# Two-layer hybrid trunk: DeltaNet's triangular solve on VectorE, taps and gates on ScalarE, mixer outputs token-major

## The chip, the cores and the metric

The kernel runs on one core of a Trainium2 chip. The metric is the device time of one execution in microseconds; the median of the runs counts. Engine names follow the profile: PE is TensorE's matmul (PEld its weight load), DVE VectorE, ACT ScalarE, POOL GpSimd, SP SyncE.

## The reference

Two layers of a trunk run on 384 tokens of width 1024: 128 prompt tokens and 256 latents. Each sub-layer is an RMS norm, a shift and scale from a conditioning vector (adaLN), the sub-layer, and a gated residual. Layer 0 mixes with two groups of heads side by side, HGRN2 and gated DeltaNet, both forward and backward; layer 1 is attention. Both end in an MLP of width 4096. What matters here is layer 0's mixer, cut:

```python
q_a, f_fw, f_bw, i_a, g_a, qkv_b, g_b, ... = split(h @ w_in)
f = lb + (1 - lb) * sigmoid(f_raw)                      # HGRN2 forget gates, per direction
o_a = rmsnorm(oa_f + oa_b, gn_a) * silu(g_a)            # HGRN2 output
qkv = silu(short_conv(qkv_b, conv_w))                   # 5 taps, centred
q_b, k_b = l2norm(q_b) * 128**-0.5, l2norm(k_b)
A = where(strict, (k * beta) @ k.T * L, 0)              # in chunks of 32 tokens
u = triangular_solve(I + A, v * beta); w = triangular_solve(I + A, k * beta * exp(g))
o_b = rmsnorm(ob_f + ob_b, gn_b) * silu(g_b)            # DeltaNet output
out = concat(o_a, o_b) @ w_out
```

## The kernel before, in words

**Precision.** Weights arrive as float32 and are split in a high part (`hi`, by ACT, L211) and a low part (`lo` = weight minus `hi`, L212, by DVE or, for blocks listed in `ON_POOL`, by POOL). Each product is three matmuls per 128 rows: hi by hi, hi by lo, lo by hi (L647 to L649 for blocks laid out feature-major, 128x384; L674 to L676 and L689 to L691 for token-major ones, 512 and 256 columns). A block's weights come in two halves of 512 KB through rings of 3 raw, 4 `whi` and 4 `wlo` tiles, so a split waits until TensorE has done with an earlier half.

**Layer 0.** First comes a preparation: the adaLN vectors, the norm, and `fm_group`, which projects the four heads of DeltaNet's keys and the first two forget gates. Then `gdn_prep` makes the 32x32 matrices, and `gdn_solve` (L1038 to L1073) inverts them: it writes them to DRAM and reads them back so that each of 96 matrices lies on a partition (the DMAs into `s` and `sm`), runs 31 steps of two `tensor_tensor` each (L1062 a product, L1063 a subtraction; sizes w(32-w) for w = 1 to 31), and sends the result back through DRAM (`s<-sm`, `hyB<-s`). `gdn_levels` (from L1096) joins the 32-blocks to 128-blocks on TensorE, `gdn_step` (L1146 to L1177) carries the states over the tiles, and `gdn_out` (L1188, L1191) makes the outputs.

**The order.** Each engine runs its instructions in order. A string, `STEPS`, says in which order the pieces are written: `d` advances DeltaNet's chain by a step, `h` HGRN's, `a` adaLN's for later; `f`, `q`, `c`, `v`, `g` are weight blocks for forget gates, queries, conv inputs, HGRN's values and output gates; `m` is the HGRN half of `mix_out`. A scheduler then sets each engine's order from it; `ORDER` holds some matmuls back behind marked ones (`behind`).

**After a block's matmuls** its `evac` runs. For conv (`evac_conv`): two ACT copies, a first tap on DVE (L940), four multiply-adds on DVE (L942), an ACT sigmoid, two POOL products (L950, L951). For forget gates (`evac_f`): an ACT sigmoid, a DVE multiply-add (L717). HGRN's levels are DVE work (L748 to L785, among them L771 and L782) with small matmuls (L747, L759).

**The tail.** The mixers' outputs lie feature-major, 128 features by 384 tokens for each head. `mix_out` squares them (ACT, L1249), sums over features with matmuls against a column of ones (L1251; for DeltaNet also the squares of q, L1255), takes a square root and a reciprocal (L1258, L1259), spreads the result over 128 partitions by matmul (L1263), multiplies and splits in hi and lo (L1265 to L1267). `proj_residual` multiplies with `w_out` (144 matmuls of 512 columns), adds to x (L1273, L1275), `norm` (L528 to L567, transposes L555) prepares the MLP's input, and `mlp` begins (L1340). Tiles go in the order 0 (prompt), 1, 2; the MLP's first two blocks take tiles 0 and 1 first and tile 2 behind.

Of the kernel before, what the change touches and what calls it, by code (L numbers as in the profile page):

```python
# [56 lines left out]
d f3 f1 f2 d q1 a2 q0 d h a2 h a h c4 h a d h3 d c5 h a2 d h v0 h d h d v1 a d h3  # L57
c0 h3 c1 h5 d2 h d2 h d h5 g0 g1 h d h m g2 g3 a3
# [7 lines left out]
ON_POOL = {1: (0, 1), "c5": (0,), "q0": (0,)}  # L66
# [41 lines left out]
class Trunk:  # L108
# [27 lines left out]
    def load_x(self):  # L136
        nc, i = self.nc, self.i
        nc.sync.dma_start(self.x[:, 0], i["x_prompt"][0])
        for t in range(2):
            nc.sync.dma_start(self.x[:, 1 + t], i["x_sample"][0, t * P:(t + 1) * P])  # L140
# [389 lines left out]
    def norm(self, A, B, tag, ready=None):  # L530
# [4 lines left out]
        for t in range(NT):  # L535
# [15 lines left out]
            for j in range(2):  # L551
                pt = self.ps([P, 4, P], "tmp")
                hf = self.sb([P, 4, P], self.tag_hf)
                for k in range(4):
                    self.mark["T", t, j] = nc.tensor.transpose(pt[:, k], xh[j][:, k * P:(k + 1) * P], self.c["ident"])  # L555
# [7 lines left out]
                if j:  # L563
                    self.mark["A", t] = nc.scalar.activation(hi.tiles[j][:, :, c], hf, AF.Copy)
                else:
                    nc.vector.tensor_copy(hi.tiles[j][:, :, c], hf)  # L566
                self.mark["D", t] = nc.vector.tensor_sub(lo.tiles[j][:, :, c], hf, hi.tiles[j][:, :, c].bitcast(F32))  # L567
# [143 lines left out]
    def evac_f(self, d, h):  # L711
        nc = self.nc

        def f(pg):
            s = self.cvt([P, NT, P])
            nc.scalar.activation(s, pg.rearrange("p (t c) -> p t c", t=NT), AF.Sigmoid)
# [124 lines left out]
    def hgrn_out(self, t, r, Sf, Sb):  # L841
# [17 lines left out]
    def mixer_tiles(self):  # L859
# [69 lines left out]
    def evac_conv(self, n):  # L929
# [4 lines left out]
        def f(pg):  # L934
# [5 lines left out]
            nc.vector.tensor_scalar(acc, raw[:, 0:386], w(0), None, op0=ALU.mult)  # L940
# [77 lines left out]

    def gdn_qg(self, t, d):
# [14 lines left out]
    def gdn_solve(self):  # L1034
# [23 lines left out]
        e = nc.gpsimd  # L1058
# [16 lines left out]
    def gdn_levels(self, d):  # L1075
# [65 lines left out]
    def gdn_step(self, t, d, S, want):  # L1141
# [28 lines left out]
        for h in range(4):  # L1170
            self.mark["s", t, d] = nc.tensor.matmul(pu[:, h], kt[:, h], ws[:, h], start=True, stop=True)
# [9 lines left out]
    def gdn_out(self, t, w, S):  # L1181
# [3 lines left out]
        for h in range(4):  # L1185
            for d in range(2):
                last = d == 1 and S is None
                self.mark["out", t] = nc.tensor.matmul(po[:, h], w[d][:, h], self.AT_[:, t, d, h], start=(d == 0), stop=last)  # L1188
            if S is not None:
                for d in range(2):  # L1190
                    nc.tensor.matmul(po[:, h], S[d][:, h], qg[d][:, h], start=False, stop=(d == 1))  # L1191
        nc.scalar.activation(self.vt[:, t], po, AF.Copy)

    def gdn_steps(self):
# [15 lines left out]
        self.gdn_attn()  # L1210
        yield
# [12 lines left out]
    def evac_gate(self, n):  # L1224
# [3 lines left out]
        def f(pg):  # L1228
            s = self.cvt([P, T])
            nc.scalar.activation(s, pg, AF.Sigmoid)  # L1230
            nc.vector.scalar_tensor_tensor(self.sg[:, n], pg, self.prm[:, 12 + n // 4:13 + n // 4], s, op0=ALU.mult, op1=ALU.mult)
        return f

    def mix_out(self, kind, y, tag):
# [570 lines left out]
```

## Time and profile before

| | us |
|---|---|
| median of 3 runs (lowest, highest) | 1165.47 (1164.83, 1169.36) |
| profiled execution | 1165.99 |
| its span | 1164.2 |
| PE busy, share of span | 1102.8 (95%) |
| PEld busy | 940.6 (81%) |
| DVE busy | 766.5 (66%) |
| ACT busy | 493.6 (42%) |
| POOL busy | 286.7 (25%) |

The profile is of one execution with 17957 instructions; the mean granted TensorE clock was 0.978 of full speed. Busy shares are averages over stages of different kinds: the MLP and attention after layer 0's mixer take the larger part of the span, and their share covers what happens in the mixer. The chain of waits and the busy times by stage tell them apart.

### The profile page before, as it was taken

Reading aid. Unit: us, or ns where it says so; the run is one execution under the profiler, and the core shown is the slowest. Engines: PE = TensorE matmul, PEld = TensorE weight load, DVE = VectorE, ACT = ScalarE, POOL = GpSimd, SP = SyncE. Lnnn points to the kernel's source line nnn. Section 1 sums busy time; section 2 is a strip of 40 time slices with the busy share of each in tenths; the row PEclk is TensorE's granted clock in tenths of the full one; section 3 lists DMA queues with packets and bytes.
Section 4 is the critical chain, followed back from the end, with each engine's and each line's share of the span. In section 5 each row is a group of like instructions: output and inputs, shape, how many; then the busy total and the mean of one; then the engine's idle time right before and its main releaser. Section 6 shows DMA issues by size and latency. Waiting matters only on the chain.

```text
span 1164.2 us, 17957 instructions
## 1 busy us (share of the span) xinstructions
PE 1102.8 (95%) x6853; PEld 940.6 (81%) x6853; DVE 766.5 (66%) x1179; ACT 493.6 (42%) x845; POOL 286.7 (25%) x309
## 2 busy tenths in 40 slices
PE   6989978998899799999999999999988999999998
PEld 3868767987866698988988878888767889999987
DVE  4587699895253788885899574877757773333333
ACT  4465323442452564334334353665635543333331
POOL 0054993231210302111112133433003011111102
PEclk9989988998998899999999999999999999999999
DMA  8954625341133287776777317665623964434301
GB/s 292 281 173 110 212 94 160 103 129 35 48 127 115 73 321 246 269 234 202 234 237 222 98 34 196 177 192 143 171 74 97 340 196 139 123 118 127 109 37 55
DMA packets 142090, 184.65 MB, mean 159 GB/s; under 512 B 36803, under 2 KB 113685, under 8 KB 142005
## 3 DMA queue, kind: packets, MB, share of 16 engines
q1 hardware_dynamic: 141685, 183.44, 50.5%
q8 instruction: 54, 0.88, 0.3%
q14 instruction: 31, 0.25, 0.1%
q10 hardware_dynamic: 320, 0.07, 0.0%
HBM read 171.53 MB, written 4.61 MB: 151 GB/s over the span
## 4 chain that ended last, share of the span: by engine, by line
PE 73%; DMA 7%; DVE 7%; POOL 7%; SPq 2%; issue 2%; ACT 1%; DVEq 0%; POOLq 0%; ACTq 0%
PE tmp L1341 7%; PE tmp L1342 7%; PE tmp L1340 7%; PE acc L1326 7%; PE acc L1327 7%; PE acc L1328 7%; POOL sm L1062 2%; POOL sm L1063 2%; DMA ada<-in_ada_w 2%; PE acc L647 2%; PE acc L648 2%; PE acc L649 2%; PE acc L675 2%; PE acc L674 2%; PE po L1715 2%
## 5 line engine op out<-in xcount | busy, mean ns | idle before, releaser
L212 DVE TENSOR_TENSOR wlo<-raw,whi 128x1024 fp32r<-128x1024 f32 x192 | 240.7, 1264 | 167.1 <-ACT whi L211 161.0
L211 ACT ACTIVATE whi<-raw 128x1024 fp32r<-128x1024 f32 x198 | 206.2, 1050 | 334.1 <-PE acc L1328 202.8
L1360 POOL TENSOR_TENSOR h<-h 128x384 f32<-128x384 f32 x56 | 66.9, 1195 | 426.4 <-ACT h L1357 423.7
L1327 PE MATMUL acc<-wlo,h 128*128 128x512 f32 x380 | 148.6, 391 | 0.0
L1326 PE MATMUL acc<-whi,h 128*128 128x512 f32 x380 | 146.1, 393 | 0.0
L349 DVE SCALAR_TENSOR_TENSOR adc<-adr,scz,adc 128x1024 f32<-128x1024 f32 x98 | 126.8, 1323 | 11.7 <-DMA adr<-in_ada_w 11.6
L1328 PE MATMUL acc<-whi,h 128*128 128x512 f32 x380 | 121.2, 391 | 0.0
L1326 PEld LDWEIGHTS acc<-whi,h 128*128 128x128 f32 x380 | 71.2, 188 | 19.7 <-ACT whi L211 5.0
L1340 PE MATMUL tmp<-hyA,whi 128*128 128x384 f32 (+1 forms) x256 | 83.8, 333 | 3.2 <-DVE hyA L566 3.2
L1341 PE MATMUL tmp<-hyA,whi 128*128 128x384 f32 (+1 forms) x256 | 84.8, 332 | 0.4 <-DVE hyA L567 0.4
L1340 PE MATMUL tmp<-hyB,whi 128*128 128x384 f32 (+1 forms) x256 | 83.7, 329 | 1.2 <-DVE hyB L566 1.2
L1341 PE MATMUL tmp<-hyB,whi 128*128 128x384 f32 (+1 forms) x256 | 84.0, 329 | 0.7 <-DVE hyB L567 0.7
L1342 PE MATMUL tmp<-hyA,wlo 128*128 128x384 f32 (+1 forms) x256 | 84.6, 332 | 0.0
L1327 PEld LDWEIGHTS acc<-wlo,h 128*128 128x128 f32 x380 | 71.4, 188 | 14.5 <-DVE wlo L212 0.8
L1342 PE MATMUL tmp<-hyB,wlo 128*128 128x384 f32 (+1 forms) x256 | 82.1, 328 | 0.0
L1328 PEld LDWEIGHTS acc<-whi,h 128*128 128x128 f32 x380 | 71.0, 188 | 13.7
L647 PE MATMUL acc<-hyA,whi 128*128 128x384 f32 x208 | 73.8, 355 | 1.4 <-DVE hyB L708 1.4
L648 PE MATMUL acc<-hyA,whi 128*128 128x384 f32 x208 | 71.9, 345 | 0.0
L649 PE MATMUL acc<-hyA,wlo 128*128 128x384 f32 x208 | 71.3, 344 | 0.0
L1361 DVE TENSOR_TENSOR h<-h,h 128x384 fp32r<-128x384 f32 (+2 forms) x72 | 38.4, 535 | 41.1 <-POOL h L1360 40.4
L1340 PEld LDWEIGHTS tmp<-hyA,whi 128*128 128x128 f32 x256 | 48.4, 191 | 4.5 <-ACT km L562 3.6
L1341 PEld LDWEIGHTS tmp<-hyA,whi 128*128 128x128 f32 x256 | 49.0, 191 | 1.6 <-DVE hyA L567 0.6
(464 smaller groups left out, 2402.5 us busy)
## 6 DMA issues: line engine op xcount, KB each, us to landing
raw<-in_w_mlp SPq DMA_DIRECT2D x128, 512.0 KB, 3.9
adr<-in_ada_w SPq DMA_DIRECT2D x80, 512.0 KB, 4.6
raw<-in_w_in_ab SPq DMA_DIRECT2D x34, 512.0 KB, 5.1
ada<-in_ada_w SPq DMA_DIRECT2D x32, 256.0 KB, 5.3
raw<-in_w_qkv_na SPq DMA_DIRECT2D x32, 256.0 KB, 3.5
raw<-in_w_out_ab SPq DMA_DIRECT2D x8, 512.0 KB, 5.3
m<-gs SPq DMA_DIRECT2D x8, 512.0 KB
raw<-in_w_qkv_na SPq DMA_DIRECT2D x8, 512.0 KB
```

The lines of the kernel that those rows point to most:

```text
L211: self.nc.scalar.activation(hi, x, AF.Copy)
L212: (eng or self.nc.vector).tensor_tensor(lo, x, hi.bitcast(F32), op=ALU.subtract)
L349: nc.vector.scalar_tensor_tensor(acc[v], raw, s[v], acc[v], op0=ALU.mult, op1=ALU.add)
L647: nc.tensor.matmul(pg[n], whi(k)[:, c], hhi[:, k], start=(k == 0), stop=False)
L648: nc.tensor.matmul(pg[n], whi(k)[:, c], hlo[:, k], start=False, stop=False)
L649: nc.tensor.matmul(pg[n], wlo(k)[:, c], hhi[:, k], start=False, stop=(k == KT - 1))
L1326: nc.tensor.matmul(pg, shi, w2hi(n)[:, o], start=start, stop=False)
L1327: nc.tensor.matmul(pg, shi, w2lo(n)[:, o], start=False, stop=False)
L1328: nc.tensor.matmul(pg, slo, w2hi(n)[:, o], start=False, stop=last)
L1340: nc.tensor.matmul(pg[n], w1hi(k)[:, c], hhi[:, k, tc_], start=(k == 0), stop=False)
L1341: nc.tensor.matmul(pg[n], w1hi(k)[:, c], hlo[:, k, tc_], start=False, stop=False)
L1342: nc.tensor.matmul(pg[n], w1lo(k)[:, c], hhi[:, k, tc_], start=False, stop=(k == KT - 1))
```

## The change

It has six parts.

1. In `gdn_solve` the 62 operations go from POOL to DVE (L1062, L1063 before; L1070, L1071 after).
2. First taps (L940 before, L936 after), the forget gates' multiply-add (L717, L716) and the copies into `XT` at the start of `gdn_levels` (L1084, L1092) go from DVE to ACT.
3. POOL makes the lo part of the first halves of f1, f3, f2 and q1 too, besides those of c5, q0 and one MLP block.
4. `STEPS` is written anew: the value conv blocks c4, c5 go first, c0 and c1 later; all four gate blocks stand ahead of `m`.
5. `hgrn_out` and `gdn_out` swap the operands of their matmuls, so that outputs come token-major. A new `out_norm` norms each tile at once (squares summed along the row by ACT, the root on POOL by `pow`, a DVE product). The q part of DeltaNet's norm is made ahead in `gdn_eps`. `mix_out` is called for each tile: four transposes, a DVE product with the gates, ACT hi, DVE lo.
6. The projection, the norm behind it and the first MLP take the tiles in the order 2, 1, 0; DeltaNet's `mix_out` stands between the two halves of the projection's first two tiles (`late`), since `w_out`'s first half multiplies HGRN's outputs alone.

The diff, cut:

```diff
-d f3 f1 f2 d q1 a2 q0 d h a2 h a h c4 h a d h3 d c5 h a2 d h v0 h d h d v1 a d h3
-c0 h3 c1 h5 d2 h d2 h d h5 g0 g1 h d h m g2 g3 a3
+d3 c4 f1 f3 d a2 c5 f2 d a2 q1 q0 d h a h c0 h a h d h3 c1 d h a2 h d v0 h d h d v1 h a d h3
+d h3 d h5 d2 h d2 h d h7 g0 g1 d2 m g2 g3 a3
...
-ON_POOL = {1: (0, 1), "c5": (0,), "q0": (0,)}
+ON_POOL = {1: (0, 1), "f1": (0,), "f3": (0,), "c5": (0,), "f2": (0,), "q1": (0,), "q0": (0,)}
...
-            nc.vector.tensor_scalar(self.G[:, :, d, h], s, self.lb1[:, h:h + 1], self.lb[:, h:h + 1],
-                                    op0=ALU.mult, op1=ALU.add)
+            nc.scalar.activation(self.G[:, :, d, h], s, AF.Identity, scale=self.lb1[:, h:h + 1], bias=self.lb[:, h:h + 1])
...
-            nc.vector.tensor_scalar(acc, raw[:, 0:386], w(0), None, op0=ALU.mult)
+            nc.scalar.activation(acc, raw[:, 0:386], AF.Copy, scale=w(0))
...
-        e = nc.gpsimd
+        e = nc.vector
         for j in range(31):
...
-            nc.vector.tensor_copy(XT[r, :, d, :, r], self.XTc[d][r])
+            nc.scalar.activation(XT[r, :, d, :, r], self.XTc[d][r], AF.Copy)
...
-                self.mark["out", t] = nc.tensor.matmul(po[:, h], w[d][:, h], self.AT_[:, t, d, h], start=(d == 0), stop=last)
+                self.mark["out", t] = nc.tensor.matmul(po[:, h], self.AT_[:, t, d, h], w[d][:, h], start=(d == 0), stop=last)
...
-        nc.scalar.activation(self.vt[:, t], po, AF.Copy)
+        self.out_norm(1, t, po, self.vt[:, t])
...
+    def out_norm(self, kind, t, po, out):
+        nc = self.nc
+        ss, rs = self.sb([P, 4], "ss4"), self.sb([P, 4], "ss4")
         for h in range(4):
+            nc.scalar.activation(out[:, h], po[:, h], AF.Square, scale=P ** -0.5, accum_out=ss[:, h:h + 1])
+        if kind:
+            nc.vector.tensor_add(ss, ss, self.qe[:, t])
+        else:
+            nc.vector.tensor_scalar(ss, ss, EPS * P, None, op0=ALU.add)
+        self.rsqrt(rs, ss)
+        nc.vector.tensor_mul(out, po, rs.unsqueeze(2).broadcast_to([P, 4, P]))
...
+    def mix_out(self, kind, t, y, tag):
...
+            nc.tensor.transpose(pt[:, h], o[:, h], self.c["ident"])
+        v = self.g2([P, 4, P])
+        nc.vector.tensor_mul(v, pt, self.gates_of(kind)[:, :, c])
+        hi, lo = (y[n].tiles[kind][:, :, c] for n in range(2))
+        nc.scalar.activation(hi, v, AF.Copy)
+        nc.vector.tensor_sub(lo, v, hi.bitcast(F32))
...
+        if late:
+            for k in range(2):
+                for t in order[:2]:
+                    for c in range(2):
+                        parts[c](pg[c, t], k, t)
+                if k == 0:
+                    for t in order:
+                        late(t)
```

How it moves instructions is seen at three places. The first is the solve. On POOL, before, with the middle of the solve and the lo half of a weight block among it (`sm4` are the solve's matrices, `wlo` a lo half):

```order
L1063 TENSOR_TENSOR sm4_139_850<-sm4_139_850,sm4_140_851 96x23x9
L1062 TENSOR_TENSOR sm4_140_851<-sm4_138_845,sm4_139_850 96x220
L1063 TENSOR_TENSOR sm4_139_850<-sm4_139_850,sm4_140_851 96x22x10
L1062 TENSOR_TENSOR sm4_140_851<-sm4_138_845,sm4_139_850 96x231
L212 TENSOR_TENSOR wlo_265_1806<-raw_262_1801,whi_264_1805 128x1024
L1063 TENSOR_TENSOR sm4_139_850<-sm4_139_850,sm4_140_851 96x21x11
L1062 TENSOR_TENSOR sm4_140_851<-sm4_138_845,sm4_139_850 96x240
L1063 TENSOR_TENSOR sm4_139_850<-sm4_139_850,sm4_140_851 96x20x12
```

The same part of the solve on DVE, after (`hyB<-cv,acc` is a query block's product with its sigmoid, L707):

```order
L1070 TENSOR_TENSOR sm4_140_851<-sm4_138_845,sm4_139_850 96x256
L210 TENSOR_TENSOR wlo_252_1660<-raw_248_1653,whi_251_1659 128x1024
L1071 TENSOR_TENSOR sm4_139_850<-sm4_139_850,sm4_140_851 96x16x16
L1070 TENSOR_TENSOR sm4_140_851<-sm4_138_845,sm4_139_850 96x255
L1071 TENSOR_TENSOR sm4_139_850<-sm4_139_850,sm4_140_851 96x15x17
L1070 TENSOR_TENSOR sm4_140_851<-sm4_138_845,sm4_139_850 96x252
L1071 TENSOR_TENSOR sm4_139_850<-sm4_139_850,sm4_140_851 96x14x18
L1070 TENSOR_TENSOR sm4_140_851<-sm4_138_845,sm4_139_850 96x247
L1071 TENSOR_TENSOR sm4_139_850<-sm4_139_850,sm4_140_851 96x13x19
L1070 TENSOR_TENSOR sm4_140_851<-sm4_138_845,sm4_139_850 96x240
L707 TENSOR_TENSOR hyB_100_651<-cv_245_1645,acc_243_1595 128x3x128
L1071 TENSOR_TENSOR sm4_139_850<-sm4_139_850,sm4_140_851 96x12x20
```

The solve's operations have left POOL's queue and stand in DVE's, with lo halves and products of the weight blocks between them; L707's product, which was DVE's before too, now stands behind half of the solve.

The second place is what TensorE has in hand just before the solve's result is used (L1096 before, L1104 after, matmuls of 32x32). Before, HGRN's values (256 columns) were the last thing ahead of it:

```order
L690 MATMUL acc_329_2209<-whi_325_2201,hyA_14_129 128x256
L691 MATMUL acc_329_2209<-wlo_326_2202,hyA_13_128 128x256
L689 MATMUL acc_329_2209<-whi_325_2201,hyA_13_128 128x256
L690 MATMUL acc_329_2209<-whi_325_2201,hyA_14_129 128x256
L691 MATMUL acc_329_2209<-wlo_326_2202,hyA_13_128 128x256
L1096 MATMUL gd_142_927<-hyB_98_649,m12_120_753 32x32 x12
L1096 MATMUL gd_143_940<-hyB_98_649,m12_120_753 32x32 x12
L956 MATMUL tmp_273_1876<-ident_73,cv_272_1873 128x128 x3
```

After, it is the conv blocks c0 and c1 (384 columns, into `acc_283` and `acc_315`), with HGRN's first small matmuls (L745) about it:

```order
L647 MATMUL acc_283_1826<-hyA_16_131,whi_280_1821 128x384
L648 MATMUL acc_283_1826<-hyA_15_130,wlo_281_1822 128x384
L646 MATMUL acc_315_2069<-hyA_13_128,whi_311_2061 128x384
L647 MATMUL acc_315_2069<-hyA_14_129,whi_311_2061 128x384
L745 MATMUL hg_289_1902<-hyB_100_651,km_288_1900 32x32 x9
L1104 MATMUL gd_142_927<-hyB_98_649,m12_120_753 32x32 x12
L1104 MATMUL gd_143_940<-hyB_98_649,m12_120_753 32x32 x12
L745 MATMUL hg_289_1902<-hyB_100_651,km_288_1900 32x32 x7
```

All of the values' matmuls and nearly all of HGRN's levels now stand behind the first use of the solve. From the end of `gdn_prep` to there TensorE now has 290 matmuls of 384 columns and 18 of the adaLN's; behind it, up to the last output, 238 of 384 columns (192 before), 144 of 256 (36 before), 240 instructions of the small L757 (L759 before).

The third place is the end of the mixers on TensorE. Before, the last state update (L1171) is followed by a sum of squares (L1251) and by a gate block:

```order
L1188 MATMUL gd_462_3087<-m12_121_754,sm4_420_2849 128x128
L1171 MATMUL gd_424_2860<-g2_423_2858,g2_422_2856 128x128 x4
L1251 MATMUL hg_468_3120<-g2_469_3121,one0_3115 32x384
L647 MATMUL acc_488_3176<-hyA_13_128,whi_484_3168 128x384
L648 MATMUL acc_488_3176<-hyA_14_129,whi_484_3168 128x384
L649 MATMUL acc_488_3176<-hyA_13_128,wlo_485_3169 128x384
```

After, HGRN's last output (L845 to L848) is followed by the transposes of HGRN's normed outputs (L1265, from `hyB_100`) and at once by the projection (L673 to L675, 128x512):

```order
L845 MATMUL hg_458_3024<-hyB_99_650,hyB_100_651 128x128
L847 MATMUL hg_458_3024<-m12_102_653,hq_269_1758 128x128
L848 MATMUL hg_458_3024<-hq_437_2924,hq_269_1758 128x128
L1265 MATMUL hg_485_3186<-ident_73,hyB_100_651 128x128 x4
L673 MATMUL acc_573_3648<-whi_521_3392,hyB_481_3182 128x512
L1265 MATMUL hg_487_3195<-ident_73,hyB_100_651 128x128 x4
L1265 MATMUL hg_489_3204<-ident_73,hyB_100_651 128x128 x4
L674 MATMUL acc_573_3648<-whi_521_3392,hyB_482_3183 128x512
L675 MATMUL acc_573_3648<-wlo_522_3393,hyB_481_3182 128x512
```

The gate blocks have moved ahead of the outputs, and the matmuls of the norms' sums are gone.

More of the change, by code (lines that the diff above doesn't have):

```diff
@@ L134, in banks, with load_x @@
         self.bank = {tag: list(b) for tag, b in tags.items()}
[L136 to L140, printed above, removed]
+    def load_x(self, order=(0, 1, 2)):
+        i = self.i
+        for t in order:
+            self.nc.sync.dma_start(self.x[:, t], i["x_sample"][0, (t - 1) * P:t * P] if t else i["x_prompt"][0])
     @contextmanager
@@ L528, in rsqrt, with norm @@
         self.nc.gpsimd.tensor_tensor(out, x, self.eps[:, 4:5].broadcast_to(list(out.shape)), op=ALU.pow)
-    def norm(self, A, B, tag, ready=None):
+    def norm(self, A, B, tag, ready=None, order=(0, 1, 2)):
         nc = self.nc
@@ L534, in norm @@
         hi, lo = self.split_tiles(tag)
-        for t in range(NT):
+        for n, t in enumerate(order):
             if ready:
@@ L1017, in gdn_attn, with gdn_eps @@
                 nc.vector.tensor_mul(self.AT_[:, t, d], pk, self.AT_[:, t, d])
+    def gdn_eps(self):
+        nc = self.nc
+        pq = self.ps([P, NT, 4], "gd")
+        for h in range(4):
+            q2 = self.g2([P, NT, P])
+            nc.scalar.activation(q2, self.kq[:, :, h, 1], AF.Square, scale=(EPS * P) ** 0.5)
+            for t in range(NT):
+                nc.tensor.matmul(pq[:, t, h:h + 1], q2[:, t], self.c["ones"][:, 0:1], start=True, stop=True)
+        self.qe = self.mixc([P, NT, 4], "qe")
+        nc.vector.tensor_scalar(self.qe, pq, EPS * EPS * P, None, op0=ALU.add)
     def gdn_qg(self, t, d):
@@ L1170, in gdn_step @@
         for h in range(4):
-            self.mark["s", t, d] = nc.tensor.matmul(pu[:, h], kt[:, h], ws[:, h], start=True, stop=True)
+            nc.tensor.matmul(pu[:, h], kt[:, h], ws[:, h], start=True, stop=True)
         S2 = W[:, 1]
@@ L1297, in proj_residual, with mlp @@
         return step
-    def mlp(self, l, hh, fine=()):
+    def mlp(self, l, hh, fine=(), order=(0, 1, 2)):
         nc, i = self.nc, self.i
         hhi, hlo = hh
-        acc = [[self.ps([P, 512], "acc") for _ in range(2)] for _ in range(NT)]
+        acc = {t: [self.ps([P, 512], "acc") for _ in range(2)] for t in order}
         NB = DFF // 256
@@ L1370, in mlp @@
             if b < BEHIND:
-                first((0, 1))
+                first(tuple(sorted(order[:2])))
                 behind.append(first)
@@ L1374, in mlp @@
                     for f in behind:
-                        f((2,))
+                        f(order[2:])
             else:
@@ L1477, in layer0 @@
                 yy = Halves(y[0::2]), Halves(y[1::2])
-                self.mix_out(0, yy, "hg")
+                for t in range(NT):
+                    self.mix_out(0, t, yy, "hg")
         self.pump(100)
@@ L1482, in layer0 @@
         self.open("spo", wo=3, xh=4)
-        self.banks(acc=(2, 3, 4, 5, 0), tmp=(6, 1), mix=(7, 6))
-        self.mix_out(1, yy, "mix")
-        self.load_x()
-        step = self.proj_residual(i["w_out_ab"][0], yy, scr, (("wo", "wo"), ("wo", "m12")))
-        hh = self.norm(*m2, "hyA", step)
+        self.banks(acc=(2, 3, 4, 5, 0, 7), tmp=(6, 1))
+        order = 2, 1, 0
+        step = self.proj_residual(i["w_out_ab"][0], yy, scr, (("wo", "wo"), ("wo", "m12")), order,
+                                  lambda t: self.mix_out(1, t, yy, "tmp"))
+        self.load_x(order)
+        hh = self.norm(*m2, "hyA", step, order)
         self.dump("x0", self.x)
```

77 lines of the change are left out of this document (28 added, 49 removed), and 9 rows, old and new, of the table ORDER.

## Prediction

> **What bounds the kernel now.** I read the profile page first. Its chain that ended last, shared out by engine and then by line, looks like a kernel bound by TensorE:
>
> ```profile
> PE 73%; DMA 7%; DVE 7%; POOL 7%; SPq 2%; issue 2%; ACT 1%; DVEq 0%; POOLq 0%; ACTq 0%
> PE tmp L1341 7%; PE tmp L1342 7%; PE tmp L1340 7%; PE acc L1326 7%; PE acc L1327 7%; PE acc L1328 7%; POOL sm L1062 2%; POOL sm L1063 2%; DMA ada<-in_ada_w 2%; PE acc L647 2%; PE acc L648 2%; PE acc L649 2%; PE acc L675 2%; PE acc L674 2%; PE po L1715 2%
> ```
>
> The MLP lines (L1326 to L1342) make up most of it, and the change hardly touches them. What stands out is GpSimd (POOL), 7% in a kernel of matmuls, on L1062 and L1063: the triangular solve. So I took the chain of waits in order of time, to find where the solve begins and ends (columns: start, length, what):
>
> ```profile
> 106.78 4.57 DMA s<-g
> ...
> 116.78 1.11 POOL sm L1062
> ...
> 177.25 0.68 POOL sm L1063
> ...
> 185.72 5.32 DMA hyB<-s
> 191.09 1.60 PE gd L1096 x48
> ...
> 316.55 0.89 PE gd L1171 x8
> ```
>
> These rows cut layer 0 into stages: preparation until 106.8, a DMA round trip that lays the matrices out for the solve, the solve from 116.8 to 181, a round trip back, the DeltaNet chain from 191.1 to 316.4, and a tail until the MLP begins at 397.9. Busy time by stage:
>
> ```profile
> core 0: us, PE busy (x) PEld busy (x) DVE busy (x) ACT busy (x) POOL busy (x), PEclk, DMA share, GB/s
> 60.00:106.80 46.80, 42.63 (x220) 32.94 (x219) 41.17 (x69) 26.13 (x57) 23.50 (x21) 0.93 0.42 132
> 106.80:116.80 10.00, 10.00 (x61) 8.91 (x60) 2.73 (x4) 6.54 (x9) 3.45 (x4) 1.00 0.69 160
> 116.80:181.00 64.20, 51.13 (x532) 41.15 (x531) 54.32 (x60) 19.27 (x33) 59.84 (x72) 0.90 0.46 152
> 181.00:191.10 10.10, 9.46 (x121) 9.08 (x120) 8.00 (x14) 4.14 (x7) 1.64 (x3) 0.82 0.73 177
> 191.10:316.40 125.30, 116.86 (x1227) 104.66 (x1228) 85.39 (x156) 43.73 (x73) 32.70 (x37) 0.96 0.28 84
> 316.40:397.90 81.50, 74.90 (x306) 51.80 (x305) 43.51 (x62) 36.01 (x61) 15.75 (x13) 0.94 0.31 100
> 397.90:1164.20 766.30, 747.69 (x4060) 655.78 (x4060) 501.26 (x732) 330.58 (x558) 143.26 (x139) 1.00 0.54 169
> ```
>
> In the solve's stage POOL is busy 59.84 of 64.2 us and TensorE 51.13 at a clock of 0.90: TensorE is being given filler. The profiled execution took 1165.99 us, 1.8 more than its 1164.2 span and 0.5 above the runs' median of 1165.47; I sum against 1165.99. About 6 us (0.5%) is what a measurement can tell from no change.
>
> **The solve on VectorE.** The rows that price it, first POOL's, then DVE's in the solve's stage, in the chain's stage, and two sizes from both:
>
> ```profile
> L1062 POOL TENSOR_TENSOR sm<-sm,sm 96x31 f32<-96x31 f32 (+15 forms) x31 | 25.9, 836 | 8.4 <-DMA sm<-s 6.3
> L1063 POOL TENSOR_TENSOR sm<-sm,sm 96x31 f32<-96x31 f32 (+15 forms) x31 | 24.8, 800 | 2.2
> L212 POOL TENSOR_TENSOR wlo<-raw,whi 128x1024 fp32r<-128x1024 f32 x4 | 9.6, 2390 | 17.6 <-ACT whi L211 17.6
> ```
>
> ```profile
> L212 DVE TENSOR_TENSOR wlo<-raw,whi 128x1024 fp32r<-128x1024 f32 x7 | 11.8, 1682 | 15.0 <-ACT whi L211 15.0
> L771 DVE TENSOR_TENSOR x<-x,m 128x512 f32<-128x512 f32 x9 | 11.3, 1272 | 0.0
> ```
>
> ```profile
> L942 DVE SCALAR_TENSOR_TENSOR cv<-cr,prm,cv 128x386 f32<-128x386 f32 x20 | 13.0, 652 | 0.1
> L212 DVE TENSOR_TENSOR wlo<-raw,whi 128x1024 fp32r<-128x1024 f32 x10 | 12.1, 1218 | 6.7 <-ACT whi L211 6.5
> L771 DVE TENSOR_TENSOR x<-x,m 128x512 f32<-128x512 f32 x12 | 8.2, 689 | 0.1
> ```
>
> ```profile
> L785 DVE TENSOR_TENSOR m<-m 128x8 f32<-128x8 f32 x3 | 0.5, 153 | 0.0
> L1273 DVE TENSOR_TENSOR g<-acc,m 128x512 f32<-128x512 f32 x6 | 4.1, 688 | 8.0 <-PE acc L676 8.0
> ```
>
> On POOL the 62 operations take 50.7 us, and strangers queued among them the rest of 64.2. On DVE an operation costs 0.145 us and 1.06 ns per element (from 153 ns at 8 and 688 at 512 elements). The solve's sizes w(32-w), twice for w from 1 to 31, add up to 10,912 elements: 62 x 0.145 + 11.6 = 20.6 us, and I add 3 for handing over between dependent operations. DVE runs in order, and the order puts among them eight conv multiply-adds (8 x 0.652 = 5.2), five lo halves (5 x 1.218 = 6.1) and three products of q (1.6 by the 512-element row): 12.9. Sum 36.5; with some waiting of the lo halves for ACT I take 40. Bounds are 35 and 55, the upper one if every DVE operation is stretched as L771 is from 689 to 1272 ns.
>
> L771 is a hint of that stretch: in the solve's stage, beside a busy POOL, it took 1.85 times as long. The Trainium skill ("SBUF — State Buffer", section "Who interferes with whom") says that a DVE instruction with two SBUF inputs contends with a GpSimd instruction that reads SBUF, and that one fully blocks the other. By that rule the solve gains twice, since what stretched DVE was the solve itself, but pays again wherever POOL's remaining lo halves fall into it; the 689 against 1272 ns agree.
>
> The round trips of 10.0 and 10.1 us stay. The result's DMAs sit on SP's queue behind weight loads, and now wait there for DVE instead of POOL; the loads ahead need slots that the same lo halves free, so I see no new wait of over 2 us.
>
> **TensorE under the solve.** TensorE runs in order, so what stands ahead of the first level (L1096, now L1104) must be done too. Its prices are spacings of starts (columns: start, length):
>
> ```profile
> 328.10 0.33 PE L648 MATMUL acc<-hyA,whi 128*128 128x384 f32 x1
> 328.27 0.33 PE L649 MATMUL acc<-hyA,wlo 128*128 128x384 f32 x1
> 328.45 0.33 PE L647 MATMUL acc<-hyA,whi 128*128 128x384 f32 x1
> ```
>
> ```profile
> 193.36 0.28 PE L689 MATMUL acc<-whi,hyA 128*128 128x256 f32 x1
> 193.48 0.28 PE L690 MATMUL acc<-whi,hyA 128*128 128x256 f32 x1
> ```
>
> ```profile
> 377.21 0.39 PE L676 MATMUL acc<-m,hyB 128*128 128x512 f32 x1
> 377.44 0.40 PE L674 MATMUL acc<-whi,hyB 128*128 128x512 f32 x1
> ```
>
> ```profile
> 311.36 1.05 PE L1156 MATMUL gd<-g,m 128*128 128x128 f32 x8
> ```
>
> ```profile
> L759 PE MATMUL hg<-hq,km 128*32 128x32 f32 x256 | 4.3, 214 | 4.0 <-DVE hyB L750 2.9 <-DVE hyB L773 1.1
> ```
>
> That is 0.175 us for 384 columns, 0.12 for 256, 0.23 for 512, 0.11 for a 128-column record (1.05 less 0.16 of pipeline end, over 8; an instruction leaves two) and 0.017 for one of 32. From the end of preparation to L1104 the new order has 290 of 384 columns (50.8), 18 of the adaLN's 512 (4.1), 9 transposes (2.0) and 41 small ones (1.4): 58.3 us, at a clock of 0.95 about 62. The chain beside it is 10.0 + 40 + 10.1 = 60. I take 62 where 84.3 was.
>
> On that clock: the rows show 0.90 and 0.82 while TensorE was fed thinly, 0.96 and 1.00 when full. The Trainium skill ("TensorE: Matmul & The Clock Gate", Part 1) says that a busy array gets the full clock back within some 3.4 us and an idle one half of it. By that rule the denser stage runs near 1.00, and 58 us would replace the 62.
>
> **Preparation.** First taps and forget gates go to ACT, and two more lo halves to POOL. The rows:
>
> ```profile
> L944 ACT ACTIVATE cv<-cv 128x386 f32<-128x386 f32 x12 | 6.3, 522 | 18.2 <-DVE cv L942 18.1
> L716 ACT ACT_TABLE_LOAD x2 | 2.6, 1283 | 0.0
> L211 ACT ACTIVATE whi<-raw 128x1024 fp32r<-128x1024 f32 x34 | 35.9, 1058 | 43.4 <-PE acc L648 31.4 <-DMA raw<-in_w_in_ab 6.6 <-PE acc L690 3.9
> ```
>
> A tap costs about 0.52 on ACT, busy only 26.13 of 46.8 us there. Two table loads and a POOL half of 2.39 instead of 1.22 on DVE may fall on the path: between 0 and +5, I take +2 (108.8).
>
> **The chain's stage.** Work that lay under the solve has to go here: by the order 46 more of 384 columns (8.1), 108 more of the values' 256 (13.0), 256 more small records of the HGRN levels (4.4), 12 transposes of outputs (2.6) and the few of the q norms: 29 us. If all of it adds, 125.3 + 29 = 154. Dense, the stage holds 238 x 0.175 + 144 x 0.12 + 220 x 0.22 + 734 x 0.017 + some 12 for the rest = 132 us. TensorE was idle 8.4 of 125.3 by its busy time; I let half of that be filled: 150. DVE's share stays under it: 85.4, some 21 moved here without stretch, 8 added by norms and gates, 6 gone to ACT, in all 108.
>
> **The tail.** The 96 gate matmuls (16.8) are gone from it, and so are the sums, broadcasts and square roots of the mixers' norms. What stays: 144 matmuls of 512 columns (33.1), 12 and 16 transposes (6.2), and the norm's two waits, which no edit removes:
>
> ```profile
> 383.07 1.30 PE L555 MATMUL tmp<-ident,xh 128*128 128x128 f32 x5 [2.68 <-DVE ss L546]
> 397.93 0.48 PE L1340 MATMUL tmp<-hyA,whi 128*128 128x256 f32 x2 [3.18 <-DVE hyA L566]
> ```
>
> Sum 45.2. DeltaNet's norm and gate are covered by the first half of the projection, which needs only HGRN's outputs (72 x 0.23 = 16.6 us); without that cover they cost about 5. Bounds 42 and 50; I take 45. Tiles 2, 1, 0 instead of 0, 1, 2 I cost at nothing, since the MLP's first two blocks again run two tiles ahead of the third.
>
> **The sum.** 108.8 + 62 + 150 + 45 = 365.8 against 397.9: 32 us less, 1165.99 - 32.1 = 1134.
>
> **The rivals.** *The solve is stretched by contention.* POOL's halves of f2, q1 and q0 (2.39 each), conv products and hi splits that come late make 55 us of it: 75 instead of 62 in that stage, so 1147. For it: L771's row, and the lo halves' 15.0 us of waiting for ACT. Against: with the solve gone POOL has little to read. The rule of the Trainium skill's "SBUF — State Buffer", "Who interferes with whom", is this rival's mechanism. Chance 0.17. *TensorE fills all gaps.* The chain's stage is near its dense content, 133 instead of 150: 1117. For it: much of what moves here is filler that waits for nothing. Against: DeltaNet's chain was no shorter before. Chance 0.13. *Slower: solve and weights go in lockstep.* The DVE queue holds lo halves between the solve's operations; each waits for ACT's hi, whose slot TensorE frees, which waits for lo halves. If that is serial, a block takes 1.06 + 2.39 + 1.68 + 24 x 0.175 + 3.1 (four taps and a sigmoid) = 12.4 us, and six blocks 75: the stage takes 95, not 62, the chain's stage its full 154, preparation 3 more: 1134 + 33 + 4 + 3 = 1174. It decides once the solve takes about 74 us. For it: DVE has no slack to reorder, and HGRN's levels, which ran beside the solve (the nine L771 above), now stand behind it. Against: four slots let two blocks be split ahead. Chance 0.12.
>
> **How the numbers follow.** The forecast has the remaining 0.58. The range goes from the second rival and a faster tail, 1112, to the first with the upper bounds of preparation, tail and chain, 1162; it leaves out the lockstep. Faster by over 0.5%: 0.58 + 0.17 + 0.13, less 0.07 for upper ends that come within 0.5%: 0.81; same 0.07; slower 0.12.
>
> **What would show it.** In the new profile L1070 and L1071 stand on DVE with means near 0.3 us, and from the first to the last some 40; the first L1104 comes about 62 us after preparation's end, and the MLP's first matmul near 366. Wrong would be: DVE waiting for hi halves among L1070 (lockstep), L1070 means above 0.5 (contention), or an MLP start after 390.

## The result and the profile after

The changed kernel takes 1153.98 us (median of 6 runs, 1149.13 to 1158.77) where the kernel before took 1166.03 (6 runs): a ratio of 0.9891, 95% interval 0.9863 to 0.9919. It is faster by about 12 us, where 32 were forecast. All ratios below are to the kernel before, run in the same group on the same chip, with disturbed runs left out.

Differences to the changed kernel are less certain than the intervals say. The kernel before took 1166 us in the group of the changed kernel's runs and 1170 to 1171 (medians) in the later groups, in which the changed kernel was not run again, so a difference taken from two ratios can be off by some 4 us. A profile shows one execution: the stage behind the MLP's start, the same code in all, varied from 766.3 to 775.0 us between profiles.

The profiled execution took 1153.83 us, 1.8 more than its span. Its busy times by stage, cut at the same events as before (result of preparation sent to DRAM, solve begun, solve ended, first level, last DeltaNet output, MLP under way):

```profile
core 0: us, PE busy (x) PEld busy (x) DVE busy (x) ACT busy (x) POOL busy (x), PEclk, DMA share, GB/s
60.00:116.20 56.20, 42.02 (x203) 32.42 (x202) 47.23 (x65) 33.85 (x73) 32.11 (x29) 0.85 0.36 120
116.20:124.20 8.00, 8.00 (x49) 7.93 (x48) 1.37 (x2) 4.91 (x7) 3.22 (x4) 1.00 0.45 93
124.20:165.60 41.40, 40.69 (x237) 33.60 (x236) 39.52 (x80) 19.21 (x29) 12.55 (x9) 1.00 0.59 191
165.60:177.30 11.70, 9.49 (x119) 8.23 (x118) 9.94 (x17) 3.96 (x7) 0.02 (x1) 1.00 0.84 240
177.30:325.20 147.90, 142.69 (x1654) 130.45 (x1655) 103.50 (x186) 63.61 (x115) 34.84 (x36) 0.97 0.31 96
325.20:383.00 57.80, 46.66 (x217) 38.52 (x215) 32.53 (x56) 24.65 (x68) 17.13 (x11) 0.90 0.36 116
383.00:1152.00 769.00, 748.99 (x4056) 658.23 (x4056) 498.59 (x730) 329.48 (x556) 143.48 (x138) 0.99 0.53 167
```

Beside the forecast's terms, in us:

| stage | before | forecast | after |
|---|---|---|---|
| until preparation's end | 106.8 | 108.8 | 116.2 |
| round trip, solve, round trip | 84.3 | 62 | 61.1 |
| DeltaNet's chain | 125.3 | 150 | 147.9 |
| tail | 81.5 | 45 | 57.8 |
| rest | 766.3 | 766.3 | 769.0 |

Two terms carry the miss: preparation, 7.4 us over the forecast, and the tail, 12.8 over. The two terms in between came out within 2.1 us. The first matmul of the first level shows what ended the second term (start, length, what, idle time before it and its cause):

```profile
177.27 2.52 PE L1104 MATMUL gd<-hyB,m 32*32 32x32 f32 x48 [2.21 <-DMA hyB<-s]
```

TensorE had done what stands ahead of it and waited 2.21 us for the solve's result. It was busy 58.2 of the 61.1 us, at a clock of 1.00: the chain through the solve set the stage, and TensorE's own work was nearly as long.

**The solve.** VectorE's groups in the solve's stage (count, busy us, mean ns, idle time before):

```profile
L1071 DVE TENSOR_TENSOR sm<-sm,sm 96x31 f32<-96x31 f32 (+15 forms) x31 | 15.2, 490 | 0.7
L1070 DVE TENSOR_TENSOR sm<-sm,sm 96x31 f32<-96x31 f32 (+15 forms) x31 | 14.2, 459 | 0.8
```

29.4 us of busy time, where 20.6 had been worked out, with 3 more for handing over. The excess is in a few long operations. One of them, with what POOL did at that moment (start, length, what):

```profile
130.18 0.33 DVE L1071 TENSOR_TENSOR sm<-sm,sm 96x175 f32<-96x175 f32 x1
130.54 2.48 DVE L1070 TENSOR_TENSOR sm<-sm,sm 96x192 f32<-96x192 f32 x1
133.06 0.50 DVE L1071 TENSOR_TENSOR sm<-sm,sm 96x192 f32<-96x192 f32 x1
```

```profile
130.41 2.40 POOL L210 TENSOR_TENSOR wlo<-raw,whi 128x1024 fp32r<-128x1024 f32 x1 [6.32 <-ACT whi L209]
```

An operation of 192 elements, 0.35 us elsewhere, lasts until the lo half that began 0.13 us earlier on POOL is done. It is not slowed by a factor; it stands. That is the rule of the Trainium skill, "SBUF — State Buffer", section "Who interferes with whom", in its strict form, and the 2.48 beside 2.40 us agree with it. Two such stops behind lo halves make about 4.2 of the 8.8 us of excess, and three operations of 1.40 to 1.51 us beside POOL's products L739 about 3.1.

**The preparation.** VectorE's conv multiply-adds in it, before and after:

```profile
L942 DVE SCALAR_TENSOR_TENSOR cv<-cr,prm,cv 128x386 f32<-128x386 f32 x15 | 12.5, 835 | 0.4
```

```profile
L938 DVE SCALAR_TENSOR_TENSOR cv<-cr,prm,cv 128x386 f32<-128x386 f32 x23 | 24.2, 1051 | 3.1 <-ACT cv L936 2.5
```

Eight more, those of c4, and each longer: 11.7 us. (With POOL's old list of lo halves, a run below, the 23 take 18.7 us, so nearly half of the 11.7 goes with the new list.) Moving the first taps away saved VectorE about 0.5 us each. TensorE waits in that stage:

```profile
PE acc L646 <- ACT cv L715: 6.6, 1, 6.6
PE tmp L952 <- POOL cv L946: 4.1, 1, 4.1
```

The first wait is for PSUM. A forget gate's sigmoid has to free it, and in ACT's queue that sigmoid stands behind c4's, which waits 5.4 us for c4's multiply-adds on VectorE and then for a load of ACT's table (1.28 us; eight of them in this stage, six before).

**The tail.** From TensorE's and ACT's timelines around DeltaNet's last output (at the end of a line: idle time before it, and what ended it):

```profile
280.93 1.14 PE L845 MATMUL hg<-hyB,hyB 128*128 128x128 f32 x8
```

```profile
325.24 0.28 ACT L1250 ACTIVATE hyB<-gd 128x128 f32<-128x128 f32 x1 [2.19 <-PE gd L1196]
326.26 0.29 ACT L1250 ACTIVATE hyB<-hg 128x128 f32<-128x128 f32 x1
328.61 1.01 POOL L526 TENSOR_TENSOR ss<-ss,eps 128x4 f32<-128x4 f32 x1 [0.94 <-DVE ss L1254]
330.49 0.46 PE L845 MATMUL hg<-hyB,hyB 128*128 128x128 f32 x2 [4.01 <-DVE ss L1254]
338.73 0.79 PE L673 MATMUL acc<-whi,hyB 128*128 128x512 f32 x1 [3.26 <-ACT hyB L1269]
```

TensorE began HGRN's outputs (L845) at 280.9 and had two of the three tiles done at 291.4. ACT squares the first of them at 326.3, right after DeltaNet's last output, because ACT's queue held HGRN's squares behind DeltaNet's. Until then the two PSUM banks of HGRN stay taken, so the third tile's outputs wait until 330.5, and the projection, which takes that tile first, begins at 338.7, 13.5 us after DeltaNet's last output.

### The profile page after: what moved, and what is told of

Its sections match the earlier page's. It is cut to its first block, busy times and chain, and to the rows that moved or that the text cites. A ratio compares the mean times of both kernels' runs of the same rounds, so it can differ in the third digit from the quotient of the medians.

```text
span 1152.0 us, 18017 instructions
## 1 busy us (share of the span) xinstructions
PE 1088.1 (94%) x6861; PEld 945.6 (82%) x6861; DVE 762.0 (66%) x1216; ACT 507.2 (44%) x904; POOL 249.7 (22%) x243
## 4 chain that ended last, share of the span: by engine, by line
PE 80%; DVE 8%; DMA 5%; ACT 3%; issue 2%; POOL 1%; SPq 1%; DVEq 0%; ACTq 0%; POOLq 0%
PE tmp L1358 8%; PE tmp L1359 8%; PE tmp L1357 7%; PE acc L1343 7%; PE acc L1344 7%; PE acc L1345 7%; DMA ada<-in_ada_w 2%; DVE cv L938 2%; PE acc L1623 2%; PE acc L1624 2%; PE acc L1625 2%; PE acc L648 2%; PE acc L646 2%; PE acc L647 2%; PE acc L673 2%
## 5 line engine op out<-in xcount | busy, mean ns | idle before, releaser
L210 DVE TENSOR_TENSOR wlo<-raw,whi 128x1024 fp32r<-128x1024 f32 (+1 forms) x188 | 229.1, 1228 | 150.9 <-ACT whi L209 142.0
L646 PE MATMUL acc<-hyA,whi 128*128 128x384 f32 x208 | 75.6, 364 | 9.1 <-ACT cv L715 6.6
L647 PE MATMUL acc<-hyA,whi 128*128 128x384 f32 x208 | 72.8, 350 | 0.0
L1378 DVE TENSOR_TENSOR h<-h,h 128x384 fp32r<-128x384 f32 (+2 forms) x72 | 37.8, 526 | 41.4 <-POOL h L1377 40.8
L646 PEld LDWEIGHTS acc<-hyA,whi 128*128 128x128 f32 x208 | 41.1, 198 | 16.8 <-ACT cv L715 7.0
L1358 PEld LDWEIGHTS tmp<-hyA,whi 128*128 128x128 f32 x256 | 49.5, 193 | 3.3 <-DVE hyA L566 2.3
```

Of the source, the lines that this page charges most:

```text
L210: (eng or self.nc.vector).tensor_tensor(lo, x, hi.bitcast(F32), op=ALU.subtract)
L646: nc.tensor.matmul(pg[n], whi(k)[:, c], hhi[:, k], start=(k == 0), stop=False)
L647: nc.tensor.matmul(pg[n], whi(k)[:, c], hlo[:, k], start=False, stop=False)
L1358: nc.tensor.matmul(pg[n], w1hi(k)[:, c], hlo[:, k, tc_], start=False, stop=False)
```

## The experiments

Thirteen kernels. The first two asked what the solve is worth, the next two undid one suspected loss each. The scheduler orders all engines anew for each edit, so two kernels can differ in more than the lines shown.

**The solve back on GpSimd, all else as changed.**

```diff
-        e = nc.vector
+        e = nc.gpsimd
```

> The changed kernel with the solve back on GpSimd, all else as changed. Theory 1 (the solve is worth what its stage shows, and what was lost was lost in the preparation and in the tail): the stage from its first to its last operation goes from 41.4 back to some 60 us, since nothing else on the path covers it: 1170 to 1177 us. Theory 2 (TensorE's moved filler is now the bound under the solve, so that the engine of the solve matters little): under 8 us slower than the changed kernel, at most 1162 us.

Ratio 0.9984 (0.9960 to 1.0008), 0.0093 or 11 us above the changed kernel: between the two theories. Its stages, and its first level:

```profile
116.80:124.30 7.50, 7.50 (x44) 7.42 (x44) 0.60 (x1) 4.42 (x7) 2.49 (x2) 0.98 0.50 96
124.30:190.30 66.00, 60.80 (x529) 51.73 (x528) 45.07 (x49) 30.11 (x48) 61.64 (x74) 1.00 0.51 160
199.20:337.90 138.70, 134.96 (x1482) 121.04 (x1483) 93.09 (x168) 57.24 (x103) 29.66 (x34) 0.94 0.31 93
```

```profile
199.18 1.01 PE L1104 MATMUL gd<-hyB,m 32*32 32x32 f32 x15 [11.03 <-DMA hyB<-s]
```

The solve takes 24.6 us more, as in theory 1, but the chain's stage takes 9.2 less, since HGRN's levels now run beside the solve on a free VectorE (529 matmul records under the solve, not 237). TensorE waits 11.03 us for the solve's result, so TensorE's filler, theory 2's bound, is not the bound here; what halves the gain is that hidden work changes its place.

**The kernel before, with the solve alone on VectorE** (the same line the other way).

> The kernel before with only the solve moved to VectorE. Theory 1: DVE has HGRN's levels beside the solve there, so it gets less than the 23 us of the changed kernel, some 10 to 18: 1148 to 1156 us. Theory 2 (the solve only pays together with the new order of blocks; alone it pushes HGRN's levels back by what it wins): within 6 us of the kernel before, 1160 to 1172 us.

Ratio 1.0021 (0.9998 to 1.0045): theory 2. Its solve and its chain:

```profile
117.50:209.60 92.10, 85.91 (x1045) 72.28 (x1044) 88.07 (x177) 37.28 (x63) 24.68 (x20) 0.98 0.54 171
221.70:316.00 94.30, 77.14 (x767) 71.29 (x767) 51.70 (x95) 26.80 (x43) 16.95 (x17) 0.95 0.12 37
```

On VectorE the solve takes 92.1 us, longer than GpSimd's 64.2, because HGRN's levels stand between its operations in the same queue (88.07 us busy). The levels done there are gone from the chain's stage, which falls from 125.3 to 94.3, and DeltaNet's last output comes at the same time.

**HGRN's last steps ahead of DeltaNet's last tile.**

```diff
-d h3 d h5 d2 h d2 h d h7 g0 g1 d2 m g2 g3 a3
+d h3 d h14 g0 g1 d7 m g2 g3 a3
```

> The changed kernel with HGRN's last steps written ahead of DeltaNet's last tile, so that ACT takes HGRN's squares first. Theory 1 (the tail is long because ACT's queue holds HGRN's finished outputs behind DeltaNet's last one): the 13.5 us between DeltaNet's last output and the projection shrink to under 4, the tail from 57.8 to 46 to 50, and the time falls by 8 to 12 us, to 1142 to 1146. Theory 2 (the tail is a chain of norm, gate and split that has to run once anyway, at a low clock): the gap moves to another wait and the time falls by 3 us at most, 1151 or more.

Ratio 0.9787 (0.9746 to 0.9829), 12 us below the changed kernel (8 by the medians): theory 1. Chain and tail:

```profile
178.90:332.30 153.40, 146.27 (x1689) 134.06 (x1690) 107.43 (x195) 67.12 (x140) 38.72 (x39) 0.97 0.32 97
332.30:372.00 39.70, 36.83 (x176) 29.94 (x174) 27.52 (x45) 19.90 (x42) 9.69 (x7) 1.00 0.40 122
```

The projection's first matmul starts at 332.05, before the last DeltaNet output is finished at 332.3: the gap of 13.5 us is gone. HGRN's third outputs now lie ahead of that output, so the chain's stage is some 5 us longer. In the two profiles the MLP begins 11 us earlier.

**The first value block behind the first forget gates.**

```diff
-d3 c4 f1 f3 d a2 c5 f2 d a2 q1 q0 d
+d3 f1 f3 d a2 c4 c5 f2 d a2 q1 q0 d
```

> The changed kernel with the first value block (c4) written behind the two forget-gate blocks again. Theory 1 (its eight multiply-adds on DVE and two table loads on ACT stand in the preparation, which took 9.5 us longer): the preparation ends at 107 to 110 instead of 116.2, the solve takes 4 to 6 us longer because the multiply-adds fall into it, and the time falls by 1 to 5 us, to 1149 to 1153. Theory 2 (the preparation is long through taps on ACT and lo halves on GpSimd, whatever block comes first): it still ends after 114 us and the time is the same or longer, 1153 to 1160.

Ratio 0.9792 (0.9755 to 0.9829): theory 1 in kind, but 11.5 us (8 by the medians, 7 at the MLP's start in the profiles) instead of 1 to 5. Its stages, and its multiply-adds in the preparation:

```profile
60.00:108.40 48.40, 44.38 (x228) 33.85 (x227) 38.16 (x59) 32.54 (x70) 27.85 (x25) 0.93 0.42 137
118.10:165.00 46.90, 38.67 (x219) 31.79 (x218) 43.67 (x85) 19.26 (x31) 13.91 (x11) 0.93 0.55 177
177.10:318.00 140.90, 137.44 (x1637) 126.09 (x1638) 104.18 (x184) 62.45 (x112) 33.45 (x36) 0.99 0.31 93
```

```profile
L938 DVE SCALAR_TENSOR_TENSOR cv<-cr,prm,cv 128x386 f32<-128x386 f32 x16 | 16.2, 1012 | 2.7 <-ACT cv L936 2.2
```

Preparation ends 7.8 us earlier and the solve takes 5.5 us longer, both as theory 1 had it; the first level is no earlier than in the changed kernel (177.1 against 177.3). But the chain's stage is 7.0 us shorter. TensorE loses less in this preparation (44.38 us busy in 48.4, 42.02 in 56.2, its wait of 6.6 us gone). Little of that is work moved: the chain's stage holds 233 matmuls of 384 columns instead of 238 and 32 of the adaLN's instead of 36, by the spacings 0.175 and 0.23 us some 1.8 of the 7.0. It also runs at a clock of 0.99 instead of 0.97. Where the rest comes from stays open.

That c4's place sets the end of the preparation is seen in all eleven kernels with the new order of blocks: the six with c4 first end it between 114.7 and 118.8 us, the five with c4 behind f1 and f3 between 108.4 and 110.3.

The next four asked whether the losses are separate, and which part of the change carries the gain.

**Both edits of order.**

> The changed kernel with both edits of order: HGRN's last steps ahead of DeltaNet's last tile, and the first value block behind the first forget gates. Theory 1 (two separate losses, one in the tail and one in the preparation): the gains of about 8 us each add, 1134 to 1141 us, or 0.970 to 0.975 of the kernel before. Theory 2 (either edit only gives TensorE the same missing filler time, so that the second finds nothing left): no better than the better of the two, 1143 to 1147, or 0.978 to 0.981.

Ratio 0.9722 (0.9662 to 0.9782): theory 1. Of the 24 us that the two edits have by their ratios singly, 20 are there together, so within the intervals they add. This is the fastest kernel that does the whole work, 0.983 of the changed one by the two ratios. Its chain and tail:

```profile
177.00:327.70 150.70, 146.31 (x1672) 134.80 (x1673) 108.31 (x193) 65.95 (x137) 37.78 (x39) 0.95 0.32 98
327.70:366.30 38.60, 36.83 (x176) 29.96 (x175) 24.96 (x45) 20.58 (x43) 12.03 (x8) 1.00 0.40 125
```

**The tail's part alone**: solve, taps, forget gates, copies, GpSimd's list and `STEPS` as before; the diff, cut (`STEPS` and the forget gates are left out here):

```diff
...
-ON_POOL = {1: (0, 1), "f1": (0,), "f3": (0,), "c5": (0,), "f2": (0,), "q1": (0,), "q0": (0,)}
+ON_POOL = {1: (0, 1), "c5": (0,), "q0": (0,)}
...
-            nc.scalar.activation(acc, raw[:, 0:386], AF.Copy, scale=w(0))
+            nc.vector.tensor_scalar(acc, raw[:, 0:386], w(0), None, op0=ALU.mult)
...
-        e = nc.vector
+        e = nc.gpsimd
...
-            nc.scalar.activation(XT[r, :, d, :, r], self.XTc[d][r], AF.Copy)
+            nc.vector.tensor_copy(XT[r, :, d, :, r], self.XTc[d][r])
```

> The changed kernel with the solve on GpSimd, taps, forget gates and copies on VectorE, the old list of GpSimd halves and the old order of blocks: what is left of the change is the token-major outputs with their norms and the order of tiles. Theory 1 (the tail holds the gain that is left, because the norms' sums, broadcasts and roots are gone from TensorE): 5 to 14 us faster than the kernel before, 0.988 to 0.996. Theory 2 (the new norms' chain through ACT, GpSimd and VectorE costs as much as the matmuls that it replaces, and only moved gate blocks hide it): within 4 us of the kernel before, 0.997 to 1.003.

Ratio 0.9901 (0.9866 to 0.9935): theory 1. What this kernel keeps gives what the whole change gives (0.9891); the other parts together gain nothing that can be told from it. It keeps the token-major outputs with their norms, the order of tiles, and the changed entries of `ORDER`. These last were not in the list of the change: in `STEPS` the gate blocks g2 and g3 stand behind `m` before and after, and it is `ORDER` that no longer holds g2 back behind the last output (before it was `("out", 0)`, now `("out", 2)` for g2 and `("out", 1)` for g3). So here too the 96 gate matmuls run ahead of the last output, and this run does not tell their share from that of the norms. Its chain and tail:

```profile
191.80:335.30 143.50, 137.33 (x1363) 126.25 (x1364) 98.53 (x177) 55.73 (x114) 35.20 (x40) 0.95 0.31 96
335.30:385.10 49.80, 40.32 (x176) 32.19 (x175) 25.98 (x47) 21.42 (x51) 12.78 (x8) 0.90 0.33 106
```

In the old order of blocks two of HGRN's three tiles are squared ahead of DeltaNet's last output (at 317.8 and 319.3 us, against 335.4), and the tail is 49.8 us.

**Without the solve's 62 operations.**

```diff
-        for j in range(31):
+        for j in range(0):
```

> The changed kernel without the 62 operations of the solve (its result is left at the identity; the round trips through DRAM stay). Theory 1 (from preparation to DeltaNet's last output TensorE's work sets the end, about 209 us in both kernels, and the solve is one of several things beside it): the solve's stage shrinks by 24 us or more, but the blocks under it move behind it, and the whole falls by 3 to 10 us, to 1144 to 1151. Theory 2 (the chain through the solve sets the end): the whole falls by 20 us or more, below 1134.

Ratio 0.9709 (0.9670 to 0.9749), 21 us below the changed kernel: nearer to theory 2. The trunk's results are not computed here; only the time counts. The first level comes at 137.5, 39.8 us earlier, and half of that arrives at the end, because this lies behind it:

```profile
137.50:309.00 171.50, 167.74 (x1896) 149.11 (x1896) 125.01 (x209) 81.31 (x166) 40.74 (x43) 0.99 0.39 123
```

Here TensorE is busy 167.74 of 171.5 us. So theory 1's floor exists, but the changed kernel was not at it.

**The old order of blocks** (`STEPS` alone undone).

> The changed kernel with the order of blocks of the kernel before (STEPS alone undone). Theory 1 (the new order loses 9 us in the preparation by c4 and hides 17 us of gate blocks that stood in the tail): the preparation ends at 106 to 109, the tail is longer by what of the gate blocks comes back to it, and the whole is within 6 us of the changed kernel, 1148 to 1160. Theory 2 (the solve on VectorE pays only with its new order, as in the kernel before it paid nothing): 8 us slower than the changed kernel or more, 1162 to 1170.

Ratio 0.9977 (0.9944 to 1.0009), 10 us above the changed kernel: theory 2. As in the kernel before with its solve on VectorE, VectorE's queue then holds HGRN's levels among the solve's operations:

```profile
119.00:212.80 93.80, 89.12 (x1065) 77.35 (x1065) 89.22 (x178) 40.90 (x72) 24.35 (x23) 0.98 0.52 165
```

With the solve, taps and lists of the kernel before in this same order (the tail's part alone) it was 0.9901, so in the old order those parts lose.

The last five took the small parts, in the changed order and in the mended one.

**First taps and forget gates back on VectorE**, as changed:

> The changed kernel with first taps and forget gates back on VectorE. Theory 1 (the 9.5 us lost in the preparation are the first value block's multiply-adds in VectorE's queue, wherever its first tap runs): the preparation ends no earlier, 116 to 119 us, and the whole is the same or up to 6 us slower, 0.988 to 0.996 of the kernel before. Theory 2 (the taps on ACT stand ahead of sigmoids that free PSUM for TensorE, and so cause the loss): the preparation ends 4 us earlier or more, and the whole is at 0.985 or less.

Ratio 0.9953 (0.9930 to 0.9975): 7 us slower than the changed kernel. The preparation ends at 118.8, later, so theory 2 falls and theory 1 stands. The solve takes 57.2 us, not 41.4.

**GpSimd's old list**, as changed:

> The changed kernel with GpSimd's old list of lo halves (those of f1, f3, f2 and q1 go back to VectorE). Theory 1 (VectorE is the scarce engine in preparation and solve, and four halves of 1.22 us come back to it): 2 to 6 us slower than the changed kernel, 0.991 to 0.995 of the kernel before. Theory 2 (a lo half on GpSimd blocks VectorE for as long as it saves it): the 2.5-us operations among the solve's go, the solve gets shorter, and the whole is the same or faster, 0.984 to 0.989.

Ratio 0.9816 (0.9789 to 0.9844): 9 us faster than the changed kernel (4 by the medians), at least what theory 2 had. Its mechanism is seen in part only. No L1070 lasts longer than 1.40 us, and the conv multiply-adds of the preparation are shorter:

```profile
L938 DVE SCALAR_TENSOR_TENSOR cv<-cr,prm,cv 128x386 f32<-128x386 f32 x23 | 18.7, 815 | 2.8 <-POOL m L946 1.2 <-ACT cv L936 1.1
```

But the solve does not get shorter: it takes 43.5 us with two more lo halves in VectorE's queue, and the first level comes at 176.6 after a preparation that ends at 114.7. The chain's stage is 143.5 us, not 147.9; why was not found.

**The same two in the mended order:**

> Both edits of order, and first taps and forget gates back on VectorE. Theory 1 (VectorE is the scarce engine under the solve once the order is mended): 3 to 8 us slower than with both edits alone, 0.975 to 0.979 of the kernel before. Theory 2 (the taps matter nowhere): within 2 us of both edits alone, 0.970 to 0.974.

> Both edits of order, and GpSimd's old list of lo halves. Theory 1 (VectorE is the scarce engine): 2 to 6 us slower than with both edits alone, 0.974 to 0.977 of the kernel before. Theory 2 (GpSimd's halves block VectorE for as long as they save it): the same or faster, 0.967 to 0.972.

Ratios 0.9770 (0.9750 to 0.9790) and 0.9750 (0.9726 to 0.9775). Taps on VectorE cost 6 us there too by the ratios, theory 1, and the first level comes at 191.6 instead of 177.0. The old list costs 3 us, theory 1's side. Both intervals overlap with that of both edits. So the list's sign seems to depend on the order: the new list hurts in the changed order and does no harm, or a little good, in the mended one. Why was not settled.

**Both edits, the solve on GpSimd:**

> Both edits of order with the solve on GpSimd. Theory 1 (about half of what the solve's stage gains reaches the end, as in the changed kernel): 8 to 14 us slower than with both edits alone, 0.979 to 0.984 of the kernel before. Theory 2 (with the order mended, TensorE's work sets the end and the solve's engine matters no more): within 3 us, 0.970 to 0.975.

Ratio 0.9832 (0.9803 to 0.9862), 13 us above both edits alone: theory 1. The solve takes 69 us, not 48, the first level comes 18.2 us later and the last DeltaNet output 10.3 us later.

## Why the prediction was right and wrong

The direction was right, and the range held the time; the size was not: 12 us where 32 were forecast. By its steps:

- **The solve, 40 us: right, 41.4 measured**, partly by luck. Its operations were busy 29.4 us where 20.6 were worked out, through stops beside GpSimd's operations (2.48 us for one of 0.35). The 3 us for handing over (1.5 measured) and the 3.5 for waits (0.3 measured) made up for most of that.
- **TensorE under the solve, 62: the number right, 61.1, the reason only in part.** 62 was TensorE's content of 58.3 us at a clock of 0.95. The content was right (busy 58.2 us), but the clock was 1.00, as the clock gate's page of the Trainium skill ("TensorE: Matmul & The Clock Gate", Part 1) has it for a dense array. What set the stage was the chain beside it, 8.0 + 41.4 + 11.7 us, forecast as 60. That the two were so close made the choice harmless.
- **The chain's stage, 150: right, 147.9.** The forecast's own sum already held that the solve's gain is paid back there (22 us won, 25 lost). The runs agree from four sides: with the solve on VectorE, on GpSimd, left out, and moved without the new order, about half of what its stage gains or loses, or all of it, is given back behind it.
- **Preparation, "between 0 and +5, I take +2": failed; +9.4.** The step priced the taps, table loads and lo halves. It put the block that the new `STEPS` places first at nothing. c4's eight multiply-adds (11.7 us more on VectorE with the stretch of all of them) stood in the diff's first line; they came to lie ahead of the matrices that the solve waits for, and, through ACT's queue, ahead of the sigmoids that free PSUM. Writing c4 later ended the preparation 7.8 us earlier, as the forecast had it. The solve took 5.5 us of that back, so the first level was no earlier; the kernel was still 8 to 11.5 us faster, by a shorter chain's stage, and how is only in part known.
- **The tail, 45 us within 42 to 50: failed; 57.8.** The 96 gate matmuls and the norms' matmuls are gone as forecast. What failed is the sentence that the first half of the projection covers DeltaNet's norm because it "needs only HGRN's outputs": it does, but those were not normed. ACT's queue held their squares behind DeltaNet's last output. The order of TensorE showed HGRN's last outputs behind DeltaNet's, and the prediction read them as work, not as the head of a chain through ACT, GpSimd and VectorE. Writing HGRN's steps ahead took the tail to 39.7 us, below the forecast.
- **The rest at nothing: 2.7 us**, within what this stage varies from profile to profile.
- **The rivals.** Contention happened (29.4 us busy), but could cost the stage at most the 2.9 us that TensorE was not busy in it. No lockstep: no lo half among the solve's operations waited for ACT; VectorE's one wait of 6.6 us for a hi half ended before the first of them. TensorE filling all gaps was nearly seen only with the solve left out.
- **The range.** By the terms that the prediction names its ends are 1114 and 1159, not 1112 and 1162; the time lies within either.

With both edits of order the ratio is 0.9722, which is 1134 us on the median before, as was forecast. That is in part chance: the preparation (109.0) and the chain's stage (150.7) then agree with their terms, but from the preparation's end to the first level it takes 68 us instead of 62, and the tail 38.6 instead of 45.

## What to carry to other kernels

When code is written in another order, price for each engine not only the operations that change but what now stands ahead of the next stage's input: a block that is only filler for TensorE is eight operations on VectorE and a place in ACT's queue. Before counting something as cover, follow its inputs through every queue to the end: matmuls done at 281 us were of no use until an in-order engine got to them at 326. In these runs a stage on the critical path that also hides work gave back about half of what was taken from it, or all of it where the order put the hidden work into the same queue.

## What the runs showed of the hardware

In the changed kernel a VectorE operation with two inputs stood for the whole of a GpSimd one that began just before it: 2.48 us beside 2.40, where 0.35 is usual. A 128x24 product of VectorE (L975) took 2.35 us beside a GpSimd half of 2.34. The clock granted to TensorE in the preparation was 0.85 where it waited 6.6 us at a stretch, and 0.93 in the kernel before and with c4 later; behind that wait matmuls of 384 columns started 0.32 us apart, not 0.175, for some 5 us. Around the gap ahead of the projection the clock was 0.73:

```profile
329.70:340.00 10.30, 6.25 (x33) 5.91 (x34) 5.02 (x8) 4.50 (x12) 2.01 (x2) 0.73 0.05 7
```

With HGRN first, and that gap gone, the whole tail ran at 1.00.
